# Which engine makes the low parts of three weight chunks in a hybrid attention, SSD and MoE layer

## The chip, the core and the metric

The kernel runs on one core of one Trainium2 chip. The metric is the time of one execution in device microseconds (us). Five things work beside each other on the core: TensorE (PE in the profile, with its weight loads as PEld), VectorE (DVE), ScalarE (ACT), GpSimd (POOL), and SyncE (SP), which issues most of the DMA transfers. Each engine works through its own instructions in a fixed order, and waits between engines are made by semaphores.

## What is computed

One layer over 256 tokens of width 1024, all in float32:

```
h    = RMSNorm(x)
proj = h @ w_in          # columns: q | k | v | indexer q | indexer k | indexer weights
                         #          | ssd z | ssd xBC | ssd dt | gate_a | gate_b
y_attn = sparse attention: QK norm, rotary, indexer scores, top-k keys, softmax, values
y_ssd  = Mamba-2 SSD: conv + SiLU on xBC, chunked scan, D skip, gated group RMSNorm with z
x = x + W_out( sigmoid(gate_a) * W_a(y_attn) + sigmoid(gate_b) * W_b(y_ssd) )
x = x + HierMoE(RMSNorm(x))     # 4 groups x 8 experts, top-1 group, top-2 experts
```

The change touches only how the columns k and v, and the two halves of gate_a, of `w_in` are prepared for the product `h @ w_in`.

## The kernel before, in words

**Products in split precision.** A float32 matrix is split into a high part (the value cast to the type fp32r) and a low part (the value less its high part). A product is the sum of three passes: high by high, high by low, low by high (`PASSES`). So each matmul on a piece of weights needs that piece's high and low parts.

**Chunks.** The weights of the input projection, of the two branch outputs and of the output come as a stream of chunks, numbered as in the names: w0 is small, w1 is the indexer query, w2 is key and value, w3 the first half of gate_a (PSUM tile `ps_g` in the trace), w4 the first half of q, w5 the second half of gate_a, w6 the second half of q, w7 and w8 are gate_b (`WORDER`), w9 on are the 256-column chunks of the SSD (B and C first, then for each of four groups two chunks xs and two chunks z, named `ps_xs00` to `ps_z31` by group and number). A wide chunk has 8 parts of 128 x 512. `Chunk` (L152) loads the raw weights in transfers of 512 KB, two parts each, into four buffers "R"; then `split` (L182) makes for each part i the high part on ScalarE (`split_hi`, L174) and the low part (`split_lo`, L178) on GpSimd or VectorE. The tuple `KSP` (L1205) says which: its entry i % 4 is 1 for GpSimd, 0 for VectorE. The split parts `w_hl` of chunks 2 to 4 lie partly in buffers "A" and partly in the six buffers "S", those of the others in "S" alone. `next_w` (L241) makes the loads and splits one chunk ahead of the matmuls (`AHEAD`).

**Matmuls.** `wide_chunk` (L306) runs two tiles of 128 tokens through the 8 parts, three passes each, at L316, with the first tile three parts ahead of the second. Products with 256 columns are at L263.

**What runs beside it.** While TensorE is on the chunks, the other work of the layer is put in between: rotary and norms of the heads (`qk_tile`, L343 to L370: VectorE does the norm, GpSimd the power at L101 and the rotary products at L367 to L370), indexer and top-k on VectorE (L479 to L483), the transposes of q and k on TensorE (`psT_*`, L379), the attention products (L541 to L566), the preparation of the SSD (L666 to L695) and the SSD steps (`ps_b` at L751, exponentials `e` on ScalarE at L753, a product on VectorE at L756, then the products `py` at L771 and L774, transposes `ps_x` at L738). After this come the two branch products, the output product, the router and the expert stream (L1052 to L1134), whose weights, about 100 MB, are loaded in transfers of 1 MB; the first five of them (`we0_0` to `we0_4`) are issued early, on the same SyncE queue as the chunks.

**What sets the order.** The program is written as Python generators that are advanced in turn, but the order in which each engine gets its instructions is chosen by a scheduler with a cost model of its own, for the whole program. Only pinned instructions keep the written order. So when one instruction goes to another engine, the scheduler makes a new order, and places far behind the edit can change.

The chunks' parts are placed on engines by this line of `split`:

```python
self.split_lo(i, pool if KSP[i % 4] else dve)
```

Of the kernel before, what the change touches and what calls it, by code (L numbers as in the profile page):

```python
# [49 lines left out]
def block_kernel(ctx, tc, xin, idn, ngain, catt, cprep, cssd, cmoe, cwr, wsm, wwide, win, wgu, wdn, out, dbg=None):  # L50
    nc = tc.nc
    pe, act, dve, pool = nc.tensor, nc.scalar, nc.vector, nc.gpsimd
# [91 lines left out]
    for t, k in TORD:  # L144
        i = pe.transpose(ps_h[k // 2][:, k % 2, t * P:(t + 1) * P], x_sb[:, t, k * P:(k + 1) * P], ident)
# [6 lines left out]
    class Chunk:  # L152
# [24 lines left out]
            hl = self.hl[i]  # L177
            return eng.tensor_sub(hl[:, 1], self.raw[i], hl[:, 0].bitcast(F32))  # L178

        def split(self):  # L180
            for i in range(len(self.raw)):
                self.split_hi(i)  # L182
                self.split_lo(i, pool if KSP[i % 4] else dve)


    pin = tc.keep_in_program_order
# [52 lines left out]
    wready = [w0, w1]  # L239

    def next_w():  # L241
        i = len(wready)
        while len(wready) < min(len(wsrc), i + 1 + AHEAD) and len(wready) - used[0] < 1 + AHEAD:
            n = len(wready)
            with ExitStack() as st:
                if n == 2:
                    st.enter_context(tc.issue_after(w1_done.ins))
                wready.append(Chunk(wsrc[n][0], wsrc[n][1], f"w{n}", "RA" if n in ON_A else "RS"))
                wready[n].split()
        used[0] += 1  # L250
        return wready[used[0] - 1].hl

# [67 lines left out]
    def cm_chunk(name, src=hT_all):  # L320

        w = next_w()
        ps = pmm.tile([P, 2, T], F32, tag="mm", name="ps_" + name)
        mm3([(ps[:, b, :], pairs(w, slice(b * P, (b + 1) * P)), src) for b in range(2)])
        return ps
# [103 lines left out]
    def first_chunk():  # L429
        w0 = next_w()  # L430
        ps = pmm.tile([P, T], F32, tag="mm", name="ps_c0")
        mm3([(ps, pairs(w0, slice(0, P)), pairs(gT, slice(0, T)))])
        return ps
# [768 lines left out]
TORD = [(0, 0), (0, 1), (0, 2)] + [x for k in range(5) for x in ((1, k), (0, k + 3))] + [(1, 5), (1, 6), (1, 7)]  # L1202
NR = 4
NS = 6
KSP = (0, 1, 0, 1)  # L1205
AHEAD = 1
SMB = 3
PF1 = ("X", "X", "X", "L")
# [15 lines left out]
ATT_PER = 2  # L1224
NBUF = {"R": NR, "S": NS, "A": 2, "G": 4, "L": 4, "H": 2, "V": 1}

# [102 lines left out]
```

## Time and profile before

| what | value |
|---|---|
| time, median of 3 runs | 598.5 us (598.15 to 599.37) |
| the profiled execution, its own time | 599.61 us |
| its span in the profile | 597.8 us |
| mean granted clock of TensorE, as a share | 0.982 |
| busy in the span: PE, DVE, ACT, POOL | 558.2, 329.5, 273.7, 249.2 us |
| low parts (L178) on POOL | 107, 152.2 us in all |
| low parts (L178) on DVE | 105, 94.5 us in all |

The profiled execution is 1.1 us above the median, and its span is 1.8 us below its own time. TensorE is the bound nearly all the way, so its idle stretches are the places where time is to be had. The rest of the profile is read by place: three stretches count here, 30 to 86 us (the wide chunks), 125 to 135 us (transposes of the second half of q), and 224 to 240 us (between two SSD chunks). From about 375 us on the expert weights set the pace, by DMA.

### The profile page before, as it was taken

To read this page: it belongs to the slowest core of one execution; us is meant where nothing else is said; L and a number is where in the kernel's file an instruction comes from. 1 tells how busy PE (TensorE), PEld (TensorE's weight loads), DVE (VectorE), ACT (ScalarE), POOL (GpSimd) and SP (SyncE) were. 2 spreads that over 40 slices of the span, in tenths; PEclk is the share of its full clock that TensorE was granted. 3 is DMA by queue.
4 is the path that set the end of the run, shared out by engine and by line. 5 is a ranking of instruction groups with operands and counts; after the bars stand their busy time and mean duration, and the time that the engine had idled before them with its cause. 6 is when DMAs were issued, how large, how long until landed. Compare 5 with 4: busy or idle time off the path is not lost.

```text
span 597.8 us, 9950 instructions
## 1 busy us (share of the span) xinstructions
PE 558.2 (93%) x3605; PEld 403.4 (67%) x3605; DVE 329.5 (55%) x705; ACT 273.7 (46%) x633; POOL 249.2 (42%) x256
## 2 busy tenths in 40 slices
PE   8989999989999997999999999999998898895986
PEld 6868768789898996899777888963453352341412
DVE  4459975799995869779795656462121111210101
ACT  7457647757887778668675446410000000000001
POOL 4897595665855345555666764200000000000000
PEclk9999999999999997999999999999999997998899
DMA  6755245363345467344748589989999999999994
GB/s 265 243 164 161 93 149 178 106 198 117 114 140 175 150 249 287 104 151 135 262 146 315 179 303 375 411 332 418 419 415 413 419 418 412 416 418 420 411 412 163
DMA packets 35811, 159.27 MB, mean 266 GB/s; under 512 B 4144, under 2 KB 5808, under 8 KB 27184
## 3 DMA queue, kind: packets, MB, share of 16 engines
q1 hardware_dynamic: 34464, 157.30, 70.2%
q10 hardware_dynamic: 1296, 1.30, 0.7%
q8 instruction: 30, 0.49, 0.3%
q14 instruction: 21, 0.17, 0.1%
HBM read 157.54 MB, written 1.05 MB: 265 GB/s over the span
## 4 chain that ended last, share of the span: by engine, by line
PE 53%; DMA 21%; DVE 10%; POOL 6%; issue 5%; ACT 4%; ACTq 0%; SPq 0%; POOLq 0%; DVEq 0%
DMA we<-wgu 13%; PE ps_S L316 7%; PE ps_z L263 5%; PE ps_xs L263 5%; PE pgu L1059 4%; PE ps_g L316 4%; DMA we<-wdn 4%; PE ps_A L316 4%; PE py L1119 3%; PE ps_g L1052 3%; PE acc L1134 2%; POOL w_hl L178 2%; DVE w_hl L178 2%; DVE acc L625 2%; PE ps_o L316 2%
## 5 line engine op out<-in xcount | busy, mean ns | idle before, releaser
L178 POOL TENSOR_TENSOR w_hl<-w_raw,w_hl 128x512 fp32r<-128x512 f32 (+1 forms) x107 | 152.2, 1427 | 75.0 <-ACT w_hl L174 54.6
L174 ACT CAST w_hl<-w_raw 128x512 fp32r<-128x512 f32 (+1 forms) x212 | 126.2, 618 | 59.0 <-PE ps_S L316 20.9
L178 DVE TENSOR_TENSOR w_hl<-w_raw,w_hl 128x512 fp32r<-128x512 f32 (+1 forms) x105 | 94.5, 902 | 41.2 <-ACT w_hl L174 40.7
L1059 PE MATMUL pgu<-we,xg 128*32 128x512 f32 x512 | 62.9, 596 | 5.9 <-DMA we<-wgu 5.9
L1077 POOL TENSOR_TENSOR dc<-Dm,cmr 128x128 f32<-128x128 f32 x16 | 6.1, 401 | 147.1 <-DVE Dm L982 132.5
L263 PE MATMUL ps_xs<-hT,w_hl 128*128 128x256 f32 x384 | 51.8, 289 | 0.0
L263 PE MATMUL ps_z<-hT,w_hl 128*128 128x256 f32 x384 | 51.5, 286 | 0.0
L316 PE MATMUL ps_g<-w_hl,gT 128*128 128x512 f32 x192 | 49.2, 400 | 1.7 <-POOL w_hl L178 1.5
L263 PEld LDWEIGHTS ps_xs<-hT,w_hl 128*128 128x128 f32 x384 | 48.6, 195 | 2.0 <-issue 2.0
L263 PEld LDWEIGHTS ps_z<-hT,w_hl 128*128 128x128 f32 x384 | 47.8, 191 | 1.0 <-issue 1.0
L316 PE MATMUL ps_S<-w_hl,yT 128*128 128x512 f32 x192 | 44.9, 392 | 0.0
L1059 PEld LDWEIGHTS pgu<-we,xg 128*32 128x32 f32 x512 | 15.3, 109 | 43.2 <-issue 26.8
L1055 DVE TENSOR_TENSOR xg<-ps_g,cmoe 128x512 f32<-128x512 f32 (+2 forms) x18 | 11.3, 631 | 57.3 <-PE ps_g L1052 57.3
L316 PEld LDWEIGHTS ps_g<-w_hl,gT 128*128 128x128 f32 x192 | 34.9, 188 | 10.5 <-POOL w_hl L178 1.9
L1052 PEld LDWEIGHTS ps_g<-Dm,x_sb 128*128 128x128 f32 x256 | 31.1, 191 | 15.9 <-issue 12.4
L316 PEld LDWEIGHTS ps_S<-w_hl,yT 128*128 128x128 f32 x192 | 35.7, 188 | 7.6 <-issue 0.2
L1119 PE MATMUL py<-we,aTt 128*32 128x512 f32 (+1 forms) x272 | 34.5, 629 | 3.8 <-DVE aTt L1105 2.1
L1097 DVE SCALAR_TENSOR_TENSOR ac<-th,pgu 128x256 f32<-128x256 f32 x8 | 3.4, 421 | 62.6 <-ACT th L1095 62.6
L1130 ACT COPY y<-py 128x512 f32<-128x512 f32 (+1 forms) x9 | 4.9, 539 | 64.2 <-PE py L1119 64.2
L1134 PE MATMUL acc<-y,dcT 128*128 128x512 f32 (+1 forms) x68 | 32.3, 602 | 1.7 <-DVE y L1132 1.6
L1052 PE MATMUL ps_g<-Dm,x_sb 128*128 128x128 f32 x256 | 33.6, 280 | 0.0
L1095 ACT ACTIVATE th<-pgu,rs 128x256 f32<-128x256 f32 x8 | 3.8, 474 | 62.4 <-PE pgu L1059 62.4
(308 smaller groups left out, 975.4 us busy)
## 6 DMA issues: line engine op xcount, KB each, us to landing
we<-wgu SPq DMA_DIRECT2D x42, 1024.0 KB, 14.3
w_raw<-wwide SPq DMA_DIRECT2D x60, 512.0 KB, 4.0
we<-wdn SPq DMA_DIRECT2D x25, 1024.0 KB, 13.5
w_raw<-win SPq DMA_DIRECT2D x44, 512.0 KB, 3.9
we<-wgu SPq DMA_DIRECT2D x44, 512.0 KB, 11.1
we<-wdn SPq DMA_DIRECT2D x14, 512.0 KB, 10.1
x_sb<-xin SPq DMA_DIRECT2D x2, 512.0 KB, 4.3
w_raw<-wsm SPq DMA_DIRECT2D x1, 512.0 KB, 5.6
```

Of the source, the lines that this page charges most:

```text
L174: return act.copy(self.hl[i][:, 0], self.raw[i])
L178: return eng.tensor_sub(hl[:, 1], self.raw[i], hl[:, 0].bitcast(F32))
L263: pe.matmul(ps, lhsT=lhs[k][:, a], rhs=rhs[k][:, b], start=j == 0 and k == 0 and i == 0, stop=j == len(regions) - 1 and k == KD - 1 and i ...
L316: pe.matmul(ps[t], lhsT=lhs[t][k][:, a], rhs=w[k][:, b], start=k == 0 and i == 0, stop=k == KD - 1 and i == 2)
L625: dve.scalar_tensor_tensor(acc[:, j:], ps[:, :T - j], w[:, 3 - j:4 - j], acc[:, j:], op0=ALU.mult, op1=ALU.add)
L1052: pe.matmul(ps[:, kk, :], lhsT=x1[:, t, (k + kk) * P:(k + kk + 1) * P], rhs=Dm[:, t].rearrange("p e j -> p (e j)"), start=t == 0, stop=t == 1)
L1055: dve.tensor_tensor(xg[:, ks, :], ps, fgain[:, ks].unsqueeze(2).to_broadcast([P, n, P]), op=ALU.mult)
L1059: i = pe.matmul(pgu[32 * e:32 * e + 32, :], lhsT=xg[:, k, 32 * e:32 * e + 32], rhs=wg[k][e], start=k == 0, stop=k == KD - 1, tile_position ...
L1077: pool.tensor_tensor(dc[:, t], Dm[:, t], cmr[:, t, 4 * q:4 * q + 4].unsqueeze(2).to_broadcast([P, 4, NSLOT]), op=ALU.mult)
L1119: i_py = pe.matmul(py[32 * e:32 * e + 32, :], lhsT=aTt[:, f, 32 * e:32 * e + 32], rhs=wd[2 * n + f][e][:, c], start=f == 0, stop=f == 1, t ...
L1130: act.copy(y, py)
L1134: pe.matmul(acc[t][n][:, c], lhsT=dcT[:, t * P:(t + 1) * P], rhs=y, start=False, stop=q == 7 and c.stop == 512)
```

## The change

For chunks 2, 3 and 5 the pattern (0, 1, 0, 1) becomes (0, 0, 0, 1): of the eight low parts of such a chunk GpSimd makes two (i = 3 and 7) in place of four, VectorE six. So six low parts of 128 x 512 in all go from GpSimd to VectorE: parts 1 and 5 of each of the three chunks. All other chunks keep their pattern, and the arithmetic of every part is the same.

```diff
-        def split(self):
+        def split(self, by):
             for i in range(len(self.raw)):
                 self.split_hi(i)
-                self.split_lo(i, pool if KSP[i % 4] else dve)
+                self.split_lo(i, pool if by[i % len(by)] else dve)
...
-                wready[n].split()
+                wready[n].split(KSP_FEW if n in FEW else KSP)
...
 KSP = (0, 1, 0, 1)
+KSP_FEW = (0, 0, 0, 1)
+FEW = (2, 3, 5)
```

The scheduler's order moves with it. First VectorE at the first gate chunk (names end in a running number; `w3_hl_440` holds parts 0 and 1 of that chunk, `w3_hl_441` parts 2 and 3, `w3_hl_442` to `w3_hl_445` parts 4 to 7; `st_ik` and `st_iq` are the split heads of the indexer). Before:

```order
L178 TENSOR_TENSOR w3_hl_442<-w3_raw_436,w3_hl_442 128x512
L399 TENSOR_TENSOR st_ik_345<-qn_ik_329,st_ik_345 128x64 x2
L399 TENSOR_TENSOR st_ik_372<-qn_ik_356,st_ik_372 128x64 x2
L178 TENSOR_TENSOR w3_hl_440<-w3_raw_432,w3_hl_440 128x512
L178 TENSOR_TENSOR w3_hl_441<-w3_raw_434,w3_hl_441 128x512
L390 TENSOR_TENSOR st_iq_417<-qn_iq_407,st_iq_417 128x8x64
L178 TENSOR_TENSOR w3_hl_444<-w3_raw_438,w3_hl_444 128x512
```

Now:

```order
L178 TENSOR_TENSOR w3_hl_442<-w3_raw_436,w3_hl_442 128x512
L178 TENSOR_TENSOR w3_hl_443<-w3_raw_436,w3_hl_443 128x512
L399 TENSOR_TENSOR st_ik_345<-qn_ik_329,st_ik_345 128x64 x2
L399 TENSOR_TENSOR st_ik_372<-qn_ik_356,st_ik_372 128x64 x2
L178 TENSOR_TENSOR w3_hl_440<-w3_raw_432,w3_hl_440 128x512 x2
L178 TENSOR_TENSOR w3_hl_441<-w3_raw_434,w3_hl_441 128x512
L178 TENSOR_TENSOR w3_hl_444<-w3_raw_438,w3_hl_444 128x512
L390 TENSOR_TENSOR st_iq_417<-qn_iq_407,st_iq_417 128x8x64
```

Part 1, the second of the two `w3_hl_440`, now stands on VectorE right behind part 0, and part 5 behind part 4; on GpSimd both are gone.

Then GpSimd behind the wide chunks (`rc_q1`, `rs_q1` and the writes of `qn_q1` are the rotary of the second half of q, `w9` and `w10` SSD chunks), as one piece of the difference, minus for before and plus for now:

```order
 L178 TENSOR_TENSOR w8_hl_1200<-w8_raw_1191,w8_hl_1200 128x512
-L178 TENSOR_TENSOR w9_hl_1343<-w9_raw_1338,w9_hl_1343 128x512
 L367 TENSOR_TENSOR rc_q1_1312<-qn_q1_1163,tabs_222 128x128
 L368 TENSOR_TENSOR rs_q1_1313<-qn_q1_1163,tabs_222 128x128
-L178 TENSOR_TENSOR w9_hl_1345<-w9_raw_1340,w9_hl_1345 128x512
+L178 TENSOR_TENSOR w9_hl_1343<-w9_raw_1338,w9_hl_1343 128x512
 L369 TENSOR_TENSOR qn_q1_1163<-rc_q1_1312,rs_q1_1313 128x8x8
 L370 TENSOR_TENSOR qn_q1_1163<-rc_q1_1312,rs_q1_1313 128x8x8
+L178 TENSOR_TENSOR w9_hl_1345<-w9_raw_1340,w9_hl_1345 128x512
```

The last step of that rotary now stands behind one low part of w9 and not two. On VectorE the split of the result (`st_q1`, L390) stands one low part and two top-k steps earlier.

Last TensorE between the SSD chunks xs20 and xs21 (`py_2728` and `py_2735` are SSD outputs of the group before, `ps_b` the inputs of later exponentials). Before:

```order
L263 MATMUL ps_xs20_2832<-hT1_209,w21_hl_2753 128x256 x6
L751 MATMUL ps_b_2904<-acsT_2049,iir_2052 128x256
L771 MATMUL py_2728<-e01_2635,xdt0_2610 64x256 x2
L774 MATMUL py_2728<-e01_2635,xdt0_2610 64x128 x2
L751 MATMUL ps_b_2914<-acsT_2049,iir_2052 128x256
L751 MATMUL ps_b_2904<-acsT_2049,iir_2052 128x256
L751 MATMUL ps_b_2914<-acsT_2049,iir_2052 128x256
L771 MATMUL py_2735<-e01_2636,xdt0_2610 64x256 x2
L774 MATMUL py_2735<-e01_2636,xdt0_2610 64x128 x2
L738 MATMUL ps_x_2896<-ident_67,xs10_2411 128x128 x4
L751 MATMUL ps_b_3048<-acsT_2049,iir_2052 128x256
L263 MATMUL ps_xs21_2941<-hT0_208,w22_hl_2820 128x256 x12
```

Now:

```order
L263 MATMUL ps_xs20_2832<-hT1_209,w21_hl_2752 128x256 x3
L771 MATMUL py_2728<-e01_2635,xdt0_2610 64x256 x2
L774 MATMUL py_2728<-e01_2635,xdt0_2610 64x128 x2
L263 MATMUL ps_xs20_2832<-hT1_209,w21_hl_2752 128x256 x9
L263 MATMUL ps_xs20_2832<-hT1_209,w21_hl_2753 128x256 x12
L751 MATMUL ps_b_2904<-acsT_2049,iir_2052 128x256
L751 MATMUL ps_b_2914<-acsT_2049,iir_2052 128x256
L771 MATMUL py_2735<-e01_2636,xdt0_2610 64x256 x2
L774 MATMUL py_2735<-e01_2636,xdt0_2610 64x128 x2
L738 MATMUL ps_x_2896<-ident_67,xs10_2411 128x128 x4
L263 MATMUL ps_xs21_2941<-hT0_208,w22_hl_2820 128x256 x12
L263 MATMUL ps_xs21_2941<-hT0_208,w22_hl_2821 128x256 x6
```

`py_2728` now stands 21 weight matmuls ahead of the end of xs20, and of the two pairs of `ps_b_2904` and `ps_b_2914` one stands among the matmuls of xs21.

More places move and are told here in words. The transposes `psT_q1` of the second half of q stand on TensorE behind 56 of the 256-column weight matmuls at L263, where they stood behind 86; the attention work after them moves by about as much, and the indexer products `ps_i` of the second block of queries stand 9 to 12 of the 512-column matmuls earlier. On GpSimd two low parts of w5 are gone, and the power (L101) of the second token tile of q's first half stands ahead of the low part `w6_hl_878`, where it stood behind it. The steps of the SSD up to xs20 stand 39 or 40 weight matmuls earlier on TensorE, and some of those after it 24 to 48 later. On SyncE the five early expert loads stand two chunk loads earlier, ahead of the two loads of w23. From the router on, TensorE's order is the same.

## Rows read from the trace of the kernel before

**Rows 1.** Profile page: busy time, share of the span and instructions of engines.
```profile
PE 558.2 (93%) x3605; PEld 403.4 (67%) x3605; DVE 329.5 (55%) x705; ACT 273.7 (46%) x633; POOL 249.2 (42%) x256
```

**Rows 2.** PE's waits, 20 to 86 us: line, waited for, total, times, longest.
```profile
PE ps_g L316 <- POOL w_hl L178: 1.5, 1, 1.5
PE ps_q L316 <- POOL w_hl L178: 1.3, 2, 0.9
PE ps_g L316 <- DVE w_hl L178: 0.2, 1, 0.2
```

**Rows 3.** In order of time (start, length, what, [idle before]): POOL, ACT, DVE, PE, first gate chunk.
```profile
37.52 1.27 POOL L178 TENSOR_TENSOR w_hl<-w_raw,w_hl 128x512 fp32r<-128x512 f32 x1
...
34.37 2.17 ACT L174 CAST w_hl<-w_raw 128x512 fp32r<-128x512 f32 x4
...
35.15 1.70 DVE L178 TENSOR_TENSOR w_hl<-w_raw,w_hl 128x512 fp32r<-128x512 f32 x2
...
38.84 2.60 PE L316 MATMUL ps_g<-w_hl,gT 128*128 128x512 f32 x10 [1.50 <-POOL w_hl L178]
```

**Rows 4.** Low parts (L178), 20 to 76 us: ns min/median/max, first and last start.
```profile
L178 DVE TENSOR_TENSOR w_hl<-w_raw,w_hl x17: 666/809/1784, 18.4 to 74.8; 128x512 fp32r<-128x512 f32 x17
...
L178 POOL TENSOR_TENSOR w_hl<-w_raw,w_hl x17: 1266/1323/1754, 19.5 to 74.1; 128x512 fp32r<-128x512 f32 x17
```

**Rows 5.** In order of time, w5 and w6: POOL, PE.
```profile
77.94 1.73 POOL L178 TENSOR_TENSOR w_hl<-w_raw,w_hl 128x512 fp32r<-128x512 f32 x1
79.62 2.11 POOL L101 TENSOR_TENSOR ss_q<-ss_q,mhalf 128x8 f32<-128x8 f32 x1
...
79.72 4.00 PE L316 MATMUL ps_q<-w_hl,gT 128*128 128x512 f32 x16 [0.93 <-POOL w_hl L178]
84.05 2.13 PE L316 MATMUL ps_q<-w_hl,gT 128*128 128x512 f32 x8 [0.34 <-POOL w_hl L178]
```

**Rows 6.** Stretches: length; busy us (instructions) of PE, PEld, DVE, ACT, POOL; PEclk, DMA share, GB/s.
```profile
60.00:80.00 20.00, 18.88 (x84) 14.73 (x83) 19.34 (x43) 11.28 (x21) 13.91 (x12) 1.00 0.31 101
...
120.00:140.00 20.00, 17.68 (x139) 16.97 (x138) 19.83 (x45) 10.93 (x22) 11.93 (x12) 1.00 0.57 185
...
220.00:240.00 20.00, 16.98 (x119) 14.31 (x119) 18.26 (x31) 16.15 (x38) 10.25 (x11) 0.83 0.74 302
240.00:260.00 20.00, 20.00 (x156) 17.02 (x156) 16.27 (x33) 13.16 (x27) 10.63 (x10) 1.00 0.40 124
400.00:560.00 160.00, 140.28 (x996) 62.61 (x996) 26.52 (x63) 9.45 (x20) 5.31 (x14) 0.96 1.01 412
```

**Rows 7.** In order of time, second half of q: POOL, ACT, DVE, PE.
```profile
124.10 1.29 POOL L178 TENSOR_TENSOR w_hl<-w_raw,w_hl 128x512 fp32r<-128x512 f32 x1
125.35 0.77 POOL L369 TENSOR_TENSOR qn_q<-rc_q,rs_q 128x64 f32<-128x64 f32 x1
126.08 0.32 POOL L370 TENSOR_TENSOR qn_q<-rc_q,rs_q 128x64 f32<-128x64 f32 x1
...
126.43 0.62 ACT L389 CAST st_q<-qn_q 128x512 fp32r<-128x512 f32 x1 [1.49 <-POOL qn_q L370]
...
129.81 1.35 DVE L390 TENSOR_TENSOR st_q<-qn_q,st_q 128x512 fp32r<-128x512 f32 x1
...
131.22 1.09 PE L379 MATMUL psT_q<-ident,st_q 128*128 128x128 f32 x8 [2.04 <-DVE st_q L390]
132.07 3.12 PE L263 MATMUL ps_bc<-hT,w_hl 128*128 128x256 f32 x24
```

**Rows 8.** PE in order of time between xs20 and xs21, and at the chunk w23.
```profile
227.80 0.39 PE L751 MATMUL ps_b<-acsT,iir 128*128 128x256 f32 x1 [1.15 <-ACT e L753]
229.43 0.58 PE L751 MATMUL ps_b<-acsT,iir 128*128 128x256 f32 x1 [1.25 <-ACT e L753]
230.64 1.12 PE L771 MATMUL py<-e,xdt 128*64 128x256 f32 x4 [0.63 <-DVE e L756]
...
243.61 1.34 PE L263 MATMUL ps_z<-hT,w_hl 128*128 128x256 f32 x10
```

**Rows 9.** SP's queue in order of time: loads of chunks.
```profile
206.53 8.49 SPq L163 DMA_DIRECT2D w_raw<-win  x3
```

## Prediction

> **What bounds the kernel now.** I read the page first, then TensorE's waits by line, then the busy times by stretch, and at each place where TensorE idles the engines in order of time. TensorE is busy 558 us of a span of 597.8 [rows 1], so a gain can only come out of its idle stretches or of stretches in which its matmuls run slow; what GpSimd or VectorE save elsewhere is worth nothing by itself. From 400 to 560 us the DMA share is 1.01 at 412 GB/s [rows 6]: there the expert stream sets the end. It follows TensorE's earlier work, since its buffers come free only as experts are worked through, so I carry a lead that TensorE has on entering it one to one to the end; a lead lost before counts for nothing.
>
> Between 20 and 86 us, where the changed chunks are used, TensorE waits three times for a reason that touches the change: 1.5 us in the first gate chunk for a low part from GpSimd, 1.3 us in two pieces in the second half of q, 0.2 us for a low part from VectorE [rows 2]. At the key/value chunk it waits for no low part. So the direct stake is 1.5 us, and the rest is what the new order does further on: a wait of 2.04 us at the transposes of q's second half [rows 7], and the stall between xs20 and xs21. There 119 matmuls ran in 20 us, against 156 in the next 20 [rows 6]: 37 fewer, and at 3.12 us for 24 [rows 7], 0.13 us each, some 4.8 us lost. Of these 1.15 + 1.25 + 0.63 = 3.03 us are waits for the exponentials `e` [rows 8]; the rest lies in small matmuls and a granted clock of 0.83 over that stretch [rows 6], where the neighbours have 1.00.
>
> **A, the first gate chunk: -1.5 us.** Part 1's low part was made by GpSimd from 37.52 to 38.79, behind the rotary of the indexer, and TensorE went on at 38.84 [rows 3]; the wait began at 38.84 - 1.50 = 37.34. VectorE ran two low parts in 1.70 us from 35.15 [rows 3]. In the new order part 1 is the second of the pair, so its low part is there at 36.85, half a microsecond before it is needed. ScalarE's high parts don't hold it: four of them ran from 34.37 to 36.54 [rows 3], the first two done by half of that, 35.46. Part 2 follows at 36.85 + 0.85 = 37.70, behind the point where TensorE starts on part 1, and part 1 gives it at least three passes first. So the whole 1.50 goes. Bounds: 0 to -1.5.
>
> One row speaks against the term. A low part took VectorE between 0.67 and 1.78 us in this stretch, and GpSimd between 1.27 and 1.75 [rows 4]: each is slow when the other works beside it. At 1.78 each, part 1 would be ready at 35.15 + 3.56 = 38.71, and A would give 0.1 us. I hold to 0.85, since that is what the pair at that very place took, while GpSimd was on the same rotary. The Trainium skill ("Perfetto Trace Analysis", section "Optimizing Scalar/DVE Operations") says that work moved between GpSimd and VectorE might not help, since the two share a read port of SBUF; the spread from 0.67 to 1.78 agrees with it, and by it A would be the 0.1 just named.
>
> **B, the second gate chunk and the second half of q: +0.4 us.** Two low parts of w5 go to VectorE, which was busy 19.34 of 20 us from 60 to 80 [rows 6]. Six direct low parts are moved in all; those of w2 and w3 fall where VectorE has gaps, and I take them at nothing. The two here cost between 2 x 0.67 and 2 x 1.78 = 3.6 us of VectorE's time [rows 4], all of which delays the top-k beside it, and TensorE only if a weight part is late behind it. GpSimd in turn is freed of two low parts, 2 x 1.32 [rows 4], but takes the power of 2.11 us ahead of the low part that started at 77.94 and for which TensorE waited 0.93 [rows 5]. These nearly cancel, and A's lead makes TensorE come earlier by 1.5. I take 0.4 us lost. Bounds: -1.3 (both waits of q's second half gone [rows 2]) to +3.6. Cover for the lows taken at nothing in w2 is that TensorE waited there for none; without it they would cost at most 2 x 1.78 - 2 x 1.27 = 1.0 us.
>
> **C, the transposes of q's second half: -0.6 us.** TensorE reaches them 30 weight matmuls earlier, 30 x 0.13 = 3.9 us. Their input comes earlier too: one low part of 1.29 us no longer stands ahead of the rotary's last steps on GpSimd, and VectorE, which had the input ready at 126.43 + 0.62 = 127.05 but began on it at 129.81 [rows 7], has it ahead of a low part and two top-k steps, so up to 2.76 us go. That is 4.05 us, hardly more than the 3.9. The indexer products that feed the top-k stand 9 to 12 matmuls earlier as well, so VectorE may come there earlier. Between -0.2 (4.05 less 3.9) and -2.0 (the wait of 2.04 gone) I take -0.6, nearer the first, since VectorE was busy 19.83 of 20 us from 120 to 140 [rows 6]. Upper bound: +3.9, if the input is not earlier at all.
>
> **D, between xs20 and xs21: -3.0 us.** The old order put three `ps_b`, two products `py_2728` and two `py_2735` there with no weight matmul between, so TensorE sat through the latency of ScalarE's and VectorE's work on `e`. Now 21 weight matmuls, 21 x 0.13 = 2.7 us, stand behind `py_2728`, and one pair of `ps_b` has gone in among the matmuls of xs21. That covers most of the 3.03 us of waits [rows 8]; the second `py` still waits for its own `e`. The SSD steps stand about 39 weight matmuls earlier, 5 us, and the lead from A to C is 1.7, so their inputs may come late again; VectorE was busy 18.26 of 20 us there [rows 6]. I take the three waits, -3.0, and nothing for the slow matmuls. Bounds: 0 to -4.8.
>
> **Loads: 0.** The five expert loads go ahead of the two loads of w23. From the load issued at 206.53 [rows 9], five of 1.05 MB at 412 GB/s [rows 6] take 12.7 us, to 219.3, and w23's two 2.5 us more, to some 222. It was first used at 243.61 [rows 8], so even 8 us earlier there are 13 us for the split. Without that cover it would cost the 2.5 us.
>
> **Sum.** -1.5 + 0.4 - 0.6 - 3.0 = -4.7 us. The profiled execution took 599.61 us, 1.1 above the median of 598.5; so 594.9 on its scale, and 593.8 against the median. All figures below are on the median's scale.
>
> **Rivals.**
> 1. *The stall stays.* A to C come as said, but between xs20 and xs21 the chain ps_b, `e` on ScalarE, product on VectorE, py sets the time, which no order on TensorE shortens. For it: VectorE's 18.26 of 20 us. Against: 2.7 us of matmuls now cover it. -1.7, so 596.8.
> 2. *Nothing gained.* The two engines slow each other, so A gives 0.1, and the rest is lost again: D's lead is met by late inputs, C at 0. -0.1 + 0.4 = +0.3, so 598.8. It speaks for it that a low part on VectorE goes from 0.67 to 1.78 us [rows 4].
> 3. *Slower: VectorE is late with q's second half.* It has no gap between 60 and 80 us [rows 6], gets two more low parts there, and keeps the queue to the transposes full. TensorE then comes to them 3.9 us earlier and waits all of that on top of the old wait. -1.5 + 0.4 + 3.9 = +2.8, so 601.3; D would have to be 0, as the SSD's inputs wait in the same queue. It decides if the input of the transposes comes less than 3.9 - 1.1 = 2.8 us earlier, of the 4.05 hoped for.
> 4. *More.* The wait of C goes in whole and the stall's slow matmuls too: -1.5 + 0.4 - 2.0 - 4.8 = -7.9, so 590.6.
>
> That the edit doesn't do what it says is no case: the order shows the six low parts on VectorE.
>
> **How the numbers follow.** Forecast 0.38, rival 1 0.20, rival 2 0.15, rival 3 0.18, rival 4 0.09. Within 0.2% is within 1.2 us, about what a measurement of this kernel can tell from no change. Faster by more: the forecast, 1 and 4, 0.67, of which I move 0.03 to the middle, because rival 1 lies only 0.5 us beyond it. Within: 0.18. Slower: 0.18. The range begins at 590.6, rival 4, and ends at 600.6, three quarters of the way to rival 3: what lies beyond is half of rival 3 and a little at the lower end, 0.13 in all. B's own bound of +3.6 lies in rival 3's part.
>
> **What would show it.** A: in the first gate chunk no wait of TensorE for a low part on GpSimd. B: waits in the second half of q at 1.0 to 2.0 us in sum. C: a wait of 1 to 2 us at `psT_q1`. D: between xs20 and xs21 no wait above half a microsecond for `e`, and over 140 matmuls in the 20 us that hold it. The forecast is wrong if TensorE's lead at 100 us is under 0.5 us, if it loses more than 3 us at `psT_q1`, or if a new stall of that kind stands at another chunk of the SSD, which the order's rows can't tell.

## The result

| | before | after |
|---|---|---|
| time, median of 4 runs each, in turns | 598.93 us (598.15 to 599.68) | 590.42 us (590.16 to 590.85) |
| ratio, 95% interval | | 0.9855 (0.9833 to 0.9878) |
| the profiled execution, its own time | 599.61 us | 590.16 us |
| its span | 597.8 us | 588.3 us |

The changed kernel is 8.5 us faster. The forecast was 593.8, so the direction is right and the size is 1.8 times what I worked out (8.5 against 4.7); the time lies 0.2 us below the low end of the range, near rival 4.

The page of after first, its line of engines beside [rows 1]:

```profile
PE 555.8 (94%) x3605; PEld 401.1 (68%) x3605; DVE 332.1 (56%) x711; ACT 272.3 (46%) x633; POOL 240.0 (41%) x250
```

TensorE's busy time fell by 2.4 us, and the span by 9.5, so 7.1 us of the shorter span are idle time of TensorE that is gone (the span falls by 1.0 us more than the medians do; the profiled execution of before lay 0.7 us above its median). Six low parts have changed engine (x256 to x250 on POOL, x705 to x711 on DVE).

TensorE's waits by line (line, waited for, total, times, longest): from 20 to 86 us, against [rows 2], and then from 86 to 320 us.

```profile
PE ps_q L316 <- POOL w_hl L178: 2.0, 2, 1.0
```

```profile
PE ps_s L541 <- DVE mx L545: 1.7, 3, 0.8
PE py L771 <- DVE e L756: 0.2, 1, 0.2
```

The wait in the first gate chunk is gone, those in the second half of q grew from 1.3 to 2.0, and of the three waits of [rows 8] nothing is left but 0.2 us for `e`. The stretches, in the columns of [rows 6], and one that the slow matmuls make interesting:

```profile
60.00:80.00 20.00, 18.04 (x80) 13.84 (x78) 19.45 (x44) 12.07 (x23) 15.16 (x15) 1.00 0.33 104
120.00:140.00 20.00, 19.47 (x163) 19.06 (x162) 18.45 (x48) 13.58 (x36) 13.36 (x12) 1.00 0.48 159
...
220.00:240.00 20.00, 20.00 (x164) 18.14 (x163) 18.38 (x36) 15.86 (x38) 11.87 (x10) 1.00 0.54 196
...
400.00:560.00 160.00, 141.97 (x984) 63.64 (x986) 26.55 (x61) 9.71 (x21) 4.55 (x12) 0.94 1.02 416
```

From 220 to 240 us TensorE now runs without a gap, 164 matmuls against 119, at a granted clock of 1.00 against 0.83. From 120 to 140 us it is 163 against 139. The expert stream is as it was, a DMA share of 1.02 at 416 GB/s.

**Where the 9.5 us came from.** I added up from the traces, line by line, the times from the start of one matmul to the start of the next, from 15 us to the first matmul of the experts (398.76 us before, 389.14 after). A line's share holds its slow matmuls and the waits right behind its matmuls.

| where | lines | us |
|---|---|---|
| wide chunks (A and B) | `ps_g` -3.32, `ps_q` +1.59 | -1.7 |
| second half of q and attention (C) | `ps_bc` -0.50, `ps_s` -0.22 | -0.7 |
| the SSD (D) | `ps_b` -4.11, `ps_z` -1.53, `ps_xs` -1.14, `ps_x` -0.36, `ps_r` +0.28 | -6.9 |

With +0.24 at the indexer's products that is -9.1 of the -9.6; the rest is in small pieces. At the first expert matmul the lead was 9.6 us, and the span ended 9.5 us earlier: what TensorE gained before the expert stream went through to the end one to one, as assumed.

### The profile page after: what moved, and what is told of

Read it like the earlier page. It is cut to its first block, busy times and chain, and to the rows that moved or that the text cites. A ratio compares the mean times of both kernels' runs of the same rounds, so it can differ in the third digit from the quotient of the medians.

```text
span 588.3 us, 9924 instructions
## 1 busy us (share of the span) xinstructions
PE 555.8 (94%) x3605; PEld 401.1 (68%) x3605; DVE 332.1 (56%) x711; ACT 272.3 (46%) x633; POOL 240.0 (41%) x250
## 4 chain that ended last, share of the span: by engine, by line
PE 63%; DMA 19%; DVE 8%; issue 3%; POOL 3%; ACT 2%; SPq 0%; ACTq 0%; DVEq 0%; POOLq 0%
DMA we<-wgu 13%; PE ps_xs L263 8%; PE ps_S L316 7%; PE ps_z L263 6%; PE ps_g L316 5%; PE pgu L1059 4%; DMA we<-wdn 4%; PE ps_A L316 4%; PE py L1119 3%; PE ps_g L1052 3%; PE acc L1134 2%; PE ps_o L316 2%; PE ps_k L316 2%; PE ps_iq L316 2%; PE ps_o L263 2%
## 5 line engine op out<-in xcount | busy, mean ns | idle before, releaser
L178 POOL TENSOR_TENSOR w_hl<-w_raw,w_hl 128x512 fp32r<-128x512 f32 (+1 forms) x101 | 140.7, 1396 | 87.8 <-ACT w_hl L174 70.1
L178 DVE TENSOR_TENSOR w_hl<-w_raw,w_hl 128x512 fp32r<-128x512 f32 (+1 forms) x111 | 97.9, 889 | 36.6 <-ACT w_hl L174 36.0
L263 PE MATMUL ps_z<-hT,w_hl 128*128 128x256 f32 x384 | 51.6, 286 | 0.0
L263 PE MATMUL ps_xs<-hT,w_hl 128*128 128x256 f32 x384 | 50.7, 285 | 0.0
L263 PEld LDWEIGHTS ps_z<-hT,w_hl 128*128 128x128 f32 x384 | 47.7, 190 | 2.0 <-issue 1.8
L263 PEld LDWEIGHTS ps_xs<-hT,w_hl 128*128 128x128 f32 x384 | 47.5, 191 | 2.1 <-issue 2.1
L316 PE MATMUL ps_g<-w_hl,gT 128*128 128x512 f32 x192 | 47.8, 398 | 0.0
L1119 PE MATMUL py<-we,aTt 128*32 128x512 f32 (+1 forms) x272 | 35.7, 651 | 4.1 <-DVE aTt L1105 2.1
```

The source lines that it names most:

```text
L263: pe.matmul(ps, lhsT=lhs[k][:, a], rhs=rhs[k][:, b], start=j == 0 and k == 0 and i == 0, stop=j == len(regions) - 1 and k == KD - 1 and i ...
L316: pe.matmul(ps[t], lhsT=lhs[t][k][:, a], rhs=w[k][:, b], start=k == 0 and i == 0, stop=k == KD - 1 and i == 2)
L1119: i_py = pe.matmul(py[32 * e:32 * e + 32, :], lhsT=aTt[:, f, 32 * e:32 * e + 32], rhs=wd[2 * n + f][e][:, c], start=f == 0, stop=f == 1, t ...
```

## The experiments

The question was why the stall between xs20 and xs21 gave 6.9 us and not 3.0, and what took it away: the low parts of which chunk, by relief of an engine, by the lead that TensorE brings, or by the order that the scheduler made. Three theories were set against each other at first. T1, order: the gain of D comes with the order on TensorE, whichever edit brings it about. T2, relief: each moved low part gives a share of the gain. T3, lead: the stall goes because TensorE arrives at another time. All kernels have the change except where said; times are medians beside runs of the kernel before on the same chip, whose medians were 599.1 to 599.8.

### One chunk alone, and two

The edits are one line each, in this order: w3 alone, w5 alone, w3 and w5, w2 alone.

```diff
-FEW = (2, 3, 5)
+FEW = (3,)
```
```diff
-FEW = (2, 3, 5)
+FEW = (5,)
```
```diff
-FEW = (2, 3, 5)
+FEW = (3,5,)
```
```diff
-FEW = (2, 3, 5)
+FEW = (2,)
```

Expected of w3 alone:

> Only chunk w3 (first gate chunk) has the new pattern; TensorE's order from 60 us on is that of the kernel before, with the three ps_b and two py pairs between xs20 and xs21. Theory 1 (the gain is mostly the order, and the order hangs on w5): the wait of 1.5 us in the first gate chunk goes, the waits of 1.15, 1.25 and 0.63 us between xs20 and xs21 stay, also the 2 us at the transposes of q's second half; 1.2 to 1.7 us faster than before, about 597.3. Theory 2 (each low part taken off GpSimd gives its share): two of six parts moved, a third of 8.5, 2.8 us faster, about 596. Theory 3 (TensorE's lead moves the stall out of the way, whatever the order): 6 us or more faster, under 593.

of w5 alone:

> Only chunk w5 (second gate chunk) has the new pattern; TensorE's order from there on is that of the changed kernel. Theory 1: the wait of 1.5 us in the first gate chunk is there again, between xs20 and xs21 no wait above 0.3 us and a granted clock of 1.00; 6.5 to 7.5 us faster than before, about 592. Theory 2: a third of 8.5, 2.8 us faster, about 596. Theory 3: without the 1.5 us of lead from the first gate chunk the stall comes back in part, 3 to 5 us faster, about 595.

of both:

> Chunks w3 and w5 have the new pattern, the key/value chunk w2 not. Theories 1 and 3: TensorE waits for no low part of w2 in either kernel, so nothing is lost: within 0.6 us of the changed kernel, 589.8 to 591.0. Theory 2: two thirds of the gain, 5.7 us faster than before, about 593.

of w2 alone:

> Only chunk w2 (key and value) has the new pattern. The scheduler makes a third order of it: the transposes of q's second half stand behind 32 of the 256-column weight matmuls (before 86, changed kernel 56), and between xs20 and xs21 stands a single ps_b. Theory 1: no gain at w2 itself, the wait of 1.5 us in the first gate chunk stays; the stall between xs20 and xs21 is gone as in the changed kernel, so 4 to 7 us faster than before unless the transposes are too early now, about 593. Theory 2: 2.8 us faster, about 596. Theory 3: no lead, so the stall stays: within 1 us of before.

Measured: w3 alone 596.59 us, ratio 0.9959 (0.994 to 0.9978); w5 alone 592.82, 0.9893 (0.9869 to 0.9916); both 591.11, 0.9863 (0.9839 to 0.9887), the whole change; w2 alone 596.0, 0.9952 (0.9936 to 0.9969).

With w3 alone the wait of the first gate chunk is gone, TensorE has a lead of some 2 us from there on, and the stall stands untouched, 2.1 us earlier in time:

```profile
225.72 0.38 PE L751 MATMUL ps_b<-acsT,iir 128*128 128x256 f32 x1 [1.15 <-ACT e L753]
227.35 0.58 PE L751 MATMUL ps_b<-acsT,iir 128*128 128x256 f32 x1 [1.25 <-ACT e L753]
228.55 1.12 PE L771 MATMUL py<-e,xdt 128*64 128x256 f32 x4 [0.62 <-DVE e L756]
```

These are the waits of [rows 8], 1.15, 1.25 and 0.63 there, and the instructions around them stand in the order of before. So a lead of the size of A doesn't move the stall (T3 falls), and two low parts less on GpSimd bring no share of it. With w5 alone TensorE has the new order, the stall is gone though the wait of the first gate chunk is there (1.9 us), and the line sums of the SSD are those of after (`ps_b` -4.11, `ps_z` -1.53, `ps_xs` -1.13):

```profile
PE ps_g L316 <- POOL w_hl L178: 1.9, 1, 1.9
PE py L771 <- DVE e L756: 0.2, 1, 0.2
```

The times alone don't refuse T2 everywhere: it expected 596 for w3 alone and for w2 alone, and 596.59 and 596.0 came. It fails with w5 (596 expected alone, 593 with w3; 592.82 and 591.11 measured). A and D are thus two gains of two edits, and they nearly add up: 2.5 + 6.3 = 8.8 us of medians against 8.0 for both together. w2 gives nothing that can be told beside the two others.

w2 alone was T1's miss. It makes a third order (the transposes of q's second half behind 32 matmuls of 256 columns), which has no stall there either, but other waits. The longest from 86 to 320 us:

```profile
PE ps_c L677 <- issue: 2.1, 1, 2.1
```

Some 593 us were expected, and 596.0 came. An order can lose elsewhere what it wins at the stall.

### One low part of w5

```diff
-KSP_FEW = (0, 0, 0, 1)
-FEW = (2, 3, 5)
+KSP_FEW = (0,0,0,1,0,1,0,1)
+FEW = (5,)
```
```diff
-KSP_FEW = (0, 0, 0, 1)
-FEW = (2, 3, 5)
+KSP_FEW = (0,1,0,1,0,0,0,1)
+FEW = (5,)
```

The first moves part 1 of w5 alone to VectorE, the second part 5 alone. Expected:

> One low part alone goes from GpSimd to VectorE: part 1 of w5. TensorE's order stays that of the kernel before but for a few rows. Order theory: nothing to speak of, within 1 us of before. Relief theory (each low part off GpSimd gives its share of 8.5 us): 1.4 us faster.

> One low part alone goes from GpSimd to VectorE: part 5 of w5. With it the scheduler gives TensorE the order of the changed kernel but for a few rows. Order theory: the gain of the run with w5 alone, 6 to 6.5 us faster than before, about 592.8. Relief theory: 1.4 us faster, like part 1.

Measured: part 1 600.04 us, ratio 1.0008 (0.9991 to 1.0025), nothing; part 5 592.56, 0.9889 (0.9865 to 0.9913). The relief is the same, one low part each. With part 1 TensorE's order is that of before, row by row, and so are its larger waits from 20 to 320 us, but for 1.2 us in place of 1.5 in the first gate chunk:

```profile
PE ps_b L751 <- ACT e L753: 2.4, 2, 1.2
PE psT_q L379 <- DVE st_q L390: 2.4, 2, 2.0
```

With part 5 TensorE's order is that of after but for six rows, the transposes of q's second half stand behind 56 matmuls and not 86, and the waits are those of after, but for the first gate chunk, where the wait for GpSimd stays:

```profile
PE ps_g L316 <- POOL w_hl L178: 1.2, 1, 1.2
```

So a single low part that goes to another engine, at about 70 us, flips TensorE's order, and the order brings some 7 us, most of it at 230 us. T1 holds, with this edge: it says where the gain comes from, not what in the order makes it.

### What in the order: the rows between xs20 and xs21

Theory P: it is the row of products and `ps_b` without weight matmuls between. Tried from both sides. In the order of before (w3 alone), the second pair of `ps_b` of the next group is held until 18 matmuls of xs21 are out; then the second `py` as well:

```diff
+            if k in hook:
+                hook.pop(k)(last)
...
+                with ExitStack() as wait:
+                    if late is not None and hh:
+                        wait.enter_context(tc.issue_after(late.ins))
+                    pe.matmul(ps[:, hh, :], lhsT=iir[:, h:h + 1].to_broadcast([P, P]), rhs=acsT, start=True, stop=True)
...
+            if (g, i) == (1, 1):
+                def after_some(last):
+                    with tc.high_priority(HP[1]):
+                        ssd_e(1, 0, last)
+                hook[3] = after_some
...
```
```diff
+                def after_some(last):
+                    with tc.high_priority(HP[2]):
+                        ssd_y(0, 1, last)
+                    with tc.high_priority(HP[1]):
+                        ssd_e(1, 0, last)
...
```

In the order of after, the matmuls of xs21 are held behind all four `ps_b`, so that two `ps_b`, the second `py`, the transposes and the other two `ps_b` stand in a row without weight matmuls. It isn't the whole old row: the first `py` keeps its 21 matmuls behind it, and two of the `ps_b` come behind the second `py`, not ahead of it.

```diff
+                st_["b"] = pe.matmul(ps[:, hh, :], lhsT=iir[:, h:h + 1].to_broadcast([P, P]), rhs=acsT, start=True, stop=True)
...
-            c()
+            with ExitStack() as st:
+                if (g, i) == (1, 1):
+                    st.enter_context(tc.issue_after(st_["b"].ins))
+                c()
```

Expected:

> The kernel with w3 alone changed (old order on TensorE, 596.6 us), and in it the second pair of ps_b for the exponentials of the next group is held back until 18 matmuls of xs21 are issued, as in the changed kernel. Theory P (the stall between xs20 and xs21 is TensorE standing at ps_b for ScalarE's e, two waits of 1.15 and 1.25 us): 2.4 to 4 us faster than with w3 alone, 592.5 to 594. Theory V (the stall is VectorE's queue: the product that the second py needs ended at 230.49 us and the second half of zs10, which frees the PSUM of xs21, at 231.69 us, behind a low part, two yg and three convolution steps): the wait moves on to the py or to xs21, less than 1 us faster than with w3 alone, about 596.

> As the run before, and the second py of the group is held back behind 18 matmuls of xs21 too, so that no product stands between the end of xs20 and the matmuls of xs21 that waits for that e. Theory P: the whole stall goes, 4.5 to 6 us faster than with w3 alone, about 591.5. Theory V: xs21 itself waits for zs10 on VectorE until about 231 us on the clock of the kernel before, where it started at 233.2: at most 2 us faster than with w3 alone, about 595.

> The changed kernel, with the matmuls of xs21 held back until the fourth ps_b between xs20 and xs21 is issued. So TensorE gets the row of products that the old order had there (two ps_b, two py, ps_x, two ps_b, and then xs21), while the SSD's chain of work on ScalarE and VectorE has run as early as in the changed kernel. Theory P (the row of products on TensorE makes the stall): two waits of a microsecond or more for e come back, 2.4 to 4 us slower than the changed kernel, about 593.5. Theory C (the stall is there because the chain over ScalarE and VectorE came late against TensorE): no wait above 0.5 us there, within 1 us of the changed kernel, about 590.5.

Measured: 598.68 us, ratio 0.9979 (0.9961 to 0.9996), where w3 alone had 0.9959; 600.11, 1.0007 (0.9989 to 1.0025); and with the row in the changed kernel 590.86, 0.9858 (0.9839 to 0.9877), no loss. TensorE in order of time, in the first, the second and the third of them:

```profile
228.77 1.12 PE L778 MATMUL py<-e,xdt 128*64 128x256 f32 x4 [3.99 <-DVE e L763]
```

```profile
229.19 4.57 PE L267 MATMUL ps_xs<-hT,w_hl 128*128 128x256 f32 x20 [4.69 <-DVE zs L728]
```

```profile
224.10 5.92 PE L263 MATMUL ps_xs<-hT,w_hl 128*128 128x256 f32 x48
```

Without the `ps_b` in front of it the `py` waits for its own `e`, 3.99 us in one piece; without the `py` the matmuls of xs21 wait for VectorE. The stall isn't made by what stands in the row. VectorE and ScalarE are late there, and whatever stands next on TensorE waits for them. Theory P falls. Theory V of the expectations had the place of the wait right (the `py`, then xs21), but not the time, which came out 2.7 and 5.1 us above its 596 and 595. The third has no wait at the row; its equal time is a balance, though, as by the line sums the SSD took 1.9 us less than in after, and a wait of 1.4 us for a low part at 333.59 us took most of that back.

### Is the whole chain late? The SSD's constants earlier

Theory C: the chain of `e` is late as a whole, because the SSD's preparation starts late behind the load of its constants. In the order of before (w3 alone) that load gets its own place in memory and is issued at the kernel's start:

```diff
+    prep = ExitStack()
+    pp = prep.enter_context(tc.tile_pool(name="pp", bufs=1, side="right"))
...
-    prep = ExitStack()
-    pp = prep.enter_context(tc.tile_pool(name="pp", bufs=1))
```

The two kernels sent with it have w3 and part 5 of w5 alone (three low parts moved), without and with the earlier load:

```diff
-                wready[n].split(KSP_FEW if n in FEW else KSP)
+                wready[n].split(SPLIT.get(n, KSP))
...
+SPLIT = {3: (0, 0, 0, 1), 5: (0, 1, 0, 1, 0, 0, 0, 1)}
```

Expected:

> The kernel with w3 alone changed (596.6 us), and the load of the SSD's constants, which there is issued only when the attention's memory is free and took 3.84 us, is issued at the start of the kernel into memory of its own. TensorE's rows between xs20 and xs21 are word for word the old ones. Theory C: the SSD's chain starts earlier by what ScalarE waited for that load, 1.06 us of idle, and by up to 3 us where the load's end was waited for by others; the stall shrinks by as much, 1 to 3 us faster than with w3 alone, 593.5 to 595.5. Theory P: no change, 596.6.

> Parts 1 and 5 of w3 and part 5 of w5 alone go to VectorE, three low parts and not six. The order is that of the changed kernel but for a few rows. From the runs with part 5 of w5 alone (592.6) and w5 with both parts (592.8), whose profiles stand 1.0 us apart when the router starts, and the 1.9 us that w3 gave: 589.5 to 590.5, no slower than the changed kernel. Relief theory: half of 8.5, 4 us faster than before, 595.

> As the run before, with the load of the SSD's constants at the start of the kernel. Theory C: in the new order the chain is not late, so nothing is gained: within 0.7 us of the run before. Otherwise, if an earlier start is worth time wherever the chain stands, 1 to 3 us faster, 587 to 589.

Measured: 596.1 us, ratio 0.9947 (0.9928 to 0.9965), then 591.01, 0.9861 (0.9843 to 0.988), and 591.18, 0.9857 (0.9839 to 0.9874). In the first the stall came 1.4 us earlier than with w3 alone, with the same three waits of 1.15, 1.25 and 0.63. The chain is not late as a whole; it moves along with TensorE. Theory C falls. Three moved low parts do what six do, and no less; the earlier load brought nothing there either.

### The distance from `ps_b` to `py`

What moves along with TensorE is a round trip: TensorE makes a `ps_b`, ScalarE takes absolute values of it twice (L752 of all 256 columns, L753 of the last 128) and the exponential (L755), VectorE the product (L756), then TensorE needs the result in `py`. TensorE in order of time, before (the rows ahead of those in [rows 8], and the matmuls of xs21 behind them):

```profile
224.43 0.28 PE L751 MATMUL ps_b<-acsT,iir 128*128 128x256 f32 x1
224.54 0.87 PE L263 MATMUL ps_xs<-hT,w_hl 128*128 128x256 f32 x6
...
233.24 2.12 PE L263 MATMUL ps_xs<-hT,w_hl 128*128 128x256 f32 x9
```

and after:

```profile
215.42 0.28 PE L751 MATMUL ps_b<-acsT,iir 128*128 128x256 f32 x1
215.54 3.02 PE L263 MATMUL ps_xs<-hT,w_hl 128*128 128x256 f32 x24
218.49 0.65 PE L771 MATMUL py<-e,xdt 128*64 128x256 f32 x4
...
219.29 2.77 PE L263 MATMUL ps_xs<-hT,w_hl 128*128 128x256 f32 x21
221.90 0.40 PE L751 MATMUL ps_b<-acsT,iir 128*128 128x256 f32 x2
222.23 0.65 PE L771 MATMUL py<-e,xdt 128*64 128x256 f32 x4
```

Before, 230.64 - 224.43 = 6.2 us lie between that `ps_b` and the second `py`, with 6 weight matmuls between. After, it is 222.23 - 215.42 = 6.8 us, with 24 + 21 = 45 between, and no wait. Theory L: this distance is the cause. In the changed kernel that one `ps_b` is held until 6, 24 or 42 matmuls of xs20 are out, which leaves 42 (a control), 24 or 6 behind it:

```diff
+                with ExitStack() as wait:
+                    if late is not None and h2 and hh:
+                        wait.enter_context(tc.issue_after(late.ins))
...
-            c()
+            if (g, i) == (1, 0):
+                def after_some(last):
+                    with tc.high_priority(300):
+                        ssd_e(0, 1, last)
+                        ssd_y(0, 1)
+                hook[7] = after_some
+            with ExitStack() as st:
+                if (g, i) == (1, 1):
+                    st.enter_context(tc.issue_after(st_["py"].ins))
+                c()
...
-            steps(g, SEQ[i])
+            steps(g, {(0, 1): "xYT", (0, 2): ""}.get((g, i), SEQ[i]))
```

(`hook[1]`, `hook[4]` and `hook[7]` for 42, 24 and 6; the matmuls of xs21 are kept behind the `py` in all three.) Expected:

> The changed kernel, with one matmul held back: the last ps_b of the group whose e the second py between xs20 and xs21 needs may be issued only when 6 matmuls of xs20 are out (42 are left); xs21 is held behind that py, where it stands in the changed kernel anyway. This is the control. Theory L (the stall is the round trip from that ps_b over ScalarE and VectorE to the py, 224.43 to 230.64 us in the kernel before, 6.2 us, less what TensorE has to do meanwhile): 42 x 0.12 + 0.84 for the other py + 0.36 for ps_b = 6.2 us of work, no wait; 590 to 591. Theory C (the whole chain was late): 590 to 591 too.

> The same, with that ps_b held back until 24 matmuls of xs20 are out, 24 are left. Theory L: 24 x 0.12 + 0.84 + 0.24 = 4.0 us of work against 6.2, a wait of 2.2 us at the second py; 592 to 593.5. If the round trip is only its bare steps (0.83 + 0.86 on ScalarE, 0.68 on VectorE, and hops, about 2.7 us): no wait, 590.5. Theory C: 590.5.

> The same, with that ps_b held back until 42 matmuls of xs20 are out, 6 are left, as in the kernel before; all the rest of the SSD's chain is as early as in the changed kernel. Theory L with the whole round trip of 6.2: 6 x 0.12 + 0.36 = 1.1 us of work, waits of about 5 us and matmuls at the lower clock behind them; 595 to 597. With the bare steps of 2.7 us: a wait of 1.6 us, 592. Theory C: within 1 us of the changed kernel, 590.5.

Measured: with 42 left 590.43 us, ratio 0.9843 (0.9826 to 0.986), with 24 left 589.97, 0.9833 (0.9816 to 0.985), with 6 left 594.4, 0.9907 (0.988 to 0.9933). The control equals after. With 6 left the time is 4.0 us above the control, between what theory L gave for a full trip of 6.2 us (595 to 597) and for its bare steps (592). In the profiles TensorE is 4.7 us later than in after at the first expert matmul, and 5.2 later than in the control. With 6 left, TensorE in order of time:

```profile
220.80 0.28 PE L758 MATMUL ps_b<-acsT,iir 128*128 128x256 f32 x1
220.91 0.87 PE L267 MATMUL ps_xs<-hT,w_hl 128*128 128x256 f32 x6
221.62 0.66 PE L758 MATMUL ps_b<-acsT,iir 128*128 128x256 f32 x2
223.79 0.39 PE L758 MATMUL ps_b<-acsT,iir 128*128 128x256 f32 x1 [1.51 <-ACT e L760]
224.35 1.12 PE L778 MATMUL py<-e,xdt 128*64 128x256 f32 x4 [0.18 <-DVE e L763]
...
227.07 2.29 PE L267 MATMUL ps_xs<-hT,w_hl 128*128 128x256 f32 x9
```

So the stall is back, with the same releasers as before, when this distance is given back. The edit gives back a little more: one more `ps_b` of the next group stands ahead of the `py` than in after, and from there on the scheduler orders the rest of the SSD anew. With 24 left it does that too, and the time stays. Of the 4.7 us only 1.51 + 0.18 = 1.7 are waits. The others are in the stretch behind them (columns of [rows 6]), here with 6 left, then in after:

```profile
215.00:220.00 5.00, 5.00 (x44) 4.55 (x43) 4.97 (x7) 3.33 (x8) 4.80 (x4) 1.00 1.03 434
220.00:225.00 5.00, 3.31 (x23) 2.39 (x21) 2.77 (x6) 3.89 (x11) 1.34 (x2) 0.93 0.99 369
225.00:230.00 5.00, 5.00 (x25) 3.94 (x22) 4.51 (x10) 3.43 (x8) 1.97 (x2) 0.50 0.32 112
230.00:235.00 5.00, 5.00 (x40) 5.00 (x38) 2.28 (x4) 3.37 (x7) 3.45 (x4) 0.89 0.13 48
```

```profile
225.00:230.00 5.00, 5.00 (x46) 5.00 (x44) 4.06 (x7) 5.00 (x13) 3.49 (x4) 1.00 0.22 90
```

From 225 to 230 us TensorE is busy all five microseconds in both, but gets 25 matmuls done in place of 46, at a granted clock of 0.50 (1.2 GHz of 2.4) in place of 1.00.

With 24 left theory L had expected about 2 us of loss, and there was none (a wait of 0.9 us for `zs` at 240.52 us is the only one of the SSD in its trace). TensorE, then VectorE, with 24 left:

```profile
218.10 0.28 PE L758 MATMUL ps_b<-acsT,iir 128*128 128x256 f32 x1
...
222.41 0.65 PE L778 MATMUL py<-e,xdt 128*64 128x256 f32 x4
...
220.78 1.22 DVE L763 TENSOR_TENSOR e<-e,cb 128x512 f32<-128x512 f32 x1
```

The `py` ran without a wait, 4.3 us after its `ps_b`; VectorE's product had ended at 220.78 + 1.22 = 222.00, 3.9 us after that `ps_b`. In after it ended 5.0 us after it (219.19 + 1.22 - 215.42):

```profile
219.19 1.22 DVE L756 TENSOR_TENSOR e<-e,cb 128x512 f32<-128x512 f32 x1
```

So the 6.8 of after are the distance that TensorE left, not the trip. The trip isn't of one length either: it depends on what stands ahead of `e` in the queues. The point from which TensorE waits lies between 24 and 6 matmuls; it wasn't narrowed down.

**What this leaves of D.** Putting the distance back costs 4.7 us of the 6.9 by the profiles (4.0 by the medians). For the other 2.2 two things are seen in the traces. First, three smaller waits of before in the SSD are gone in after and with 6 left alike. From 86 to 320 us before (the first 0.63 of the 1.2 belongs to the stall):

```profile
PE py L771 <- DVE e L756: 1.2, 2, 0.6
PE ps_c L677 <- issue: 0.4, 1, 0.4
PE ps_a L687 <- DVE ahl L684: 0.3, 1, 0.3
```

Start to start, the matmuls that hold these three took 0.70, 0.57 and 0.47 us more than such a matmul takes elsewhere, 1.7 in sum. Second, the stall has 1.7 us of waits with 6 left and 3.03 before, 1.3 less, since the trip took 224.35 - 220.80 = 3.55 us, and before 6.2. ScalarE and VectorE in order of time, before:

```profile
225.44 0.46 ACT L752 ACTIVATE e<-ps_b,nacs 128x256 f32<-128x256 f32 x1
...
227.62 0.86 ACT L755 ACTIVATE e<-e 128x768 f32<-128x768 f32 x1
...
228.39 1.50 DVE L625 SCALAR_TENSOR_TENSOR acc<-ps_xs,cssd,acc 128x255 f32<-128x255 f32 x3
229.81 0.68 DVE L756 TENSOR_TENSOR e<-e,cb 128x512 f32<-128x512 f32 x1
```

and with 6 left:

```profile
221.11 0.47 ACT L759 ACTIVATE e<-ps_b,nacs 128x256 f32<-128x256 f32 x1 [1.40 <-PE ps_b L758]
...
222.64 0.84 ACT L762 ACTIVATE e<-e 128x768 f32<-128x768 f32 x1
...
223.51 0.69 DVE L763 TENSOR_TENSOR e<-e,cb 128x512 f32<-128x512 f32 x1
```

Before, the exponential ended at 227.62 + 0.86 = 228.48 and the product followed at 229.81, behind three steps of the convolution. With 6 left it ended at 223.48 and the product followed at 223.51. On ScalarE the first absolute value came 225.44 - 224.43 = 1.0 us after its `ps_b`, with 6 left 0.3. So in the old order the trip was longer by 1.3 and 0.7 us of queue. But the slow matmuls behind the waits cost more with 6 left. Start to start from 221.62 to 231.22 us, the stall there took 5.8 us more than the same matmuls take in after: 2.4 at the three `ps_b`, 0.9 at the `py`, 0.6 at the transposes, 1.9 at the matmuls of xs21. Before it took 6.2 (worked out below), 0.4 more. The two together, 1.7 and 0.4, are about the 2.2 that is missing, and no run gave either of them back by itself: the 4.7 are shown, the 2.2 only read.

## Why the prediction was right or wrong

**A, the first gate chunk: right.** Forecast -1.5, and the wait of [rows 3] is gone; w3 alone, which is A and little else, gave 1.9 us at the first expert matmul. TensorE, then VectorE, after:

```profile
36.05 3.43 PE L316 MATMUL ps_g<-w_hl,gT 128*128 128x512 f32 x14
...
34.58 2.42 DVE L178 TENSOR_TENSOR w_hl<-w_raw,w_hl 128x512 fp32r<-128x512 f32 x3 [0.92 <-ACT w_hl L174]
```

VectorE made three low parts in a row in 0.81 us each, against the 0.85 that I took. The rule of the Trainium skill ("Perfetto Trace Analysis", section "Optimizing Scalar/DVE Operations"), that work moved between GpSimd and VectorE might not help as they share a port, would have left 0.1 of A. At this place the trace doesn't bear it out: three parts in a row at 0.81 us, and the wait is gone. That a part can be slow beside the other engine the trace of before does show: the 26 low parts of 128x512 on VectorE during which GpSimd worked for less than a tenth of the time took at most 0.69 us, the 54 with GpSimd at work for over six tenths took 0.93 in the median and up to 1.81. All low parts from 20 to 76 us, against [rows 4]:

```profile
L178 DVE TENSOR_TENSOR w_hl<-w_raw,w_hl x23: 665/733/1792, 19.9 to 75.5; 128x512 fp32r<-128x512 f32 x23
...
L178 POOL TENSOR_TENSOR w_hl<-w_raw,w_hl x11: 1280/1520/1747, 19.4 to 69.9; 128x512 fp32r<-128x512 f32 x11
```

On GpSimd the median rose from 1323 to 1520 ns, on VectorE it fell from 809 to 733. The parts are not the same ones in the two kernels, so this is not shown to be a price of the move.

**B, the second gate chunk and the second half of q: small, as said.** Forecast +0.4. A and B together made -1.7 by the lines of the wide chunks, and w3 alone, which is A without B, -1.7 too (`ps_g` -1.61, `ps_q` -0.11), so B is about 0. The waits in the second half of q came to 2.0 us, 0.7 more than before and the upper end of what was said.

**C, the second half of q: the sum right, the way not.** Forecast -0.6, measured -0.7. The step said that TensorE would come only 0.1 us less early than the input and keep a wait of 1 to 2 us. But the transposes ran at 123.92, 7.3 us earlier than before, without a wait:

```profile
123.92 1.09 PE L379 MATMUL psT_q<-ident,st_q 128*128 128x128 f32 x8
```

So the input came earlier by more than the 4.05 us that I had worked out, even less A's lead of some 2 us. What came in return is the 1.7 us of waits at the attention's scores (`ps_s` for `mx`, above), 0.7 before. A stall was turned into another, and 0.6 came out by chance.

**D, the stall: the step that failed.** The mechanism was right, its size was not: forecast -3.0, bounds 0 to -4.8, measured -6.9. The step said "I take the three waits, -3.0, and nothing for the slow matmuls", and that was wrong in two ways. First, the slow matmuls go with the waits. Start to start, the three `ps_b` that hold the waits took 4.0 us more than such a matmul takes elsewhere, 1.0 more than the 3.03 of waits; the second `py` behind them 0.7 more; the transposes and the `ps_b` behind that 0.6 more; and ten matmuls of xs21 from 233 to 235 us, at a granted clock of 0.50, some 0.21 us each in place of 0.12, 0.9 more. Before, in the columns of [rows 6]:

```profile
230.00:235.00 5.00, 4.37 (x23) 3.74 (x23) 4.81 (x10) 4.61 (x12) 1.47 (x2) 0.50 0.91 356
```

That is 6.2 for the stall itself. The run with 6 matmuls left shows the same kind of loss: 1.7 us of waits, 5.8 us in the stall. Second, the three smaller waits of the SSD, 1.7 us start to start, weren't in the sum at all, and all went. 6.2 + 1.7 = 7.9, and other products of the SSD took 1.0 of it back (`py` elsewhere 0.7, `ps_r` 0.3), which leaves the 6.9 measured. The bound of -4.8, from 37 missing matmuls, was taken from one stretch of 20 us against its neighbour and so missed these.

The reason that the stall goes was seen too narrowly as well: the 21 weight matmuls behind `py_2728` are half of it. What counts is the number between the `ps_b` and the `py` that needs its `e`, 6 before and 45 after, and it could have been counted in the orders beforehand: the piece shown of TensorE's old order begins with those six.

**Loads: right**, 0; w23 was not waited for. **Rival 1** (the stall stays) and **rival 2** (nothing gained) fell with the first profile, and **rival 3** (VectorE late with q's second half) too: VectorE was busy 19.45 us of 20 between 60 and 80 us, and the transposes still had their input. **Rival 4** had the time right to 0.2 us, partly by luck: the stall's slow matmuls were right in kind, but at -4.8 too small against -6.9, and the gain of 2.0 at C, which didn't come (-0.7), made up for most of that. Its chance of 0.09 was too low: the 4.8 us of missing matmuls stood in the working, and taking the waits alone was the lower of two readings, chosen without a row that spoke for it.

## What to carry to other kernels

A gap of TensorE can cost more than its waits, here 5.8 us with 1.7 us of waits and 6.2 with 3.03: take the loss from the missing matmuls in the stretch, including those behind the gap that run at a lower granted clock, and not from the list of waits. Where a product goes out to ScalarE and VectorE and comes back, count the matmuls between the one that sends and the one that needs; here 45 and 24 covered the trip and 6 did not. And where a scheduler orders the whole program, try several small edits that make it order anew, since here moving one low part at 70 us gained 7 us, most of it at 230 us, and moving another of the same chunk nothing.

## What the runs showed of the hardware

- After a stall with 1.7 us of waits (1.51 and 0.18) TensorE's granted clock was 0.50 from 225 to 230 us, and 0.89 in the five microseconds after, with TensorE busy 5.00 us of 5 in both; from 215 to 220 us, ahead of the stall, it was 1.00. In after, without the stall, it was 1.00 from 220 to 240 us.
- From the start of that `ps_b` on TensorE, over ScalarE, to the end of VectorE's product it took 3.4 us (6 left), 3.9 (24 left), 5.0 (after) and 6.1 (before), with the same operations. Between 6 left and before the difference was read as queue on ScalarE and VectorE.
- A low part of 128x512 took VectorE at most 0.69 us where GpSimd worked for less than a tenth of its time, and 0.93 in the median, up to 1.81, where GpSimd worked for over six tenths of it (before; 26 and 54 parts).
